# A hybrid encoder trunk on one core: half B's stream tile in the place of the projection's ring, half A's first recurrence chunk starting with the work that needs no inverse, gated outputs loaded by GpSimd's queue, and bonus sums one pair later

## The chip, the cores and the metric

The kernel runs on one core of one Trainium2 chip. TensorE (PE) multiplies, VectorE (DVE), ScalarE (ACT) and GpSimd (POOL) do the element-wise work, and SyncE (SP) does little but issue transfers; ACT and POOL issue some too. The metric is the device time of one execution in microseconds.

## The reference

Two pre-norm layers, each a mixer and a SwiGLU feed-forward (FFN), then a final norm. Width 1024, 1024 tokens, FFN width 2816, all float32. The first mixer is a gated MLP beside mean pooling; the second is RWKV-7, and the change is about that one:

```python
def rwkv7_time_mix(h, mu, w_r, w_k, w_v, w_o, w0, w1, w2, a0, a1, a2, g1, g2,
                   k_k, k_a, r_k, ln_w, ln_b, v_first, vres):
    xx = jnp.pad(h, ((0, 0), (1, 0), (0, 0)))[:, :-1] - h
    xr, xw, xk, xv, xa, xg = [h + xx * mu[i] for i in range(6)]
    r = xr @ w_r
    wlog = -jax.nn.softplus(-(w0 + jnp.tanh(xw @ w1) @ w2).astype(f32)) - 0.5
    k = xk @ w_k
    v = xv @ w_v
    a = jax.nn.sigmoid(a0 + (xa @ a1) @ a2)
    g = jax.nn.sigmoid(xg @ g1) @ g2
    kk = heads(k * k_k)
    kk = kk / jnp.maximum(jnp.sqrt(jnp.sum(kk * kk, axis=-1, keepdims=True)), 1e-12)
    k = k * (1 + (a - 1) * k_a)
    ...
    # per head, over time: state = state * w + (state @ -kk) (kk * a)^T + v k^T ; y = state @ r
    y = wkv7_scan(rh, decay, kh, vh, -kk, kk * ah)
    ...  # per-head norm of y, then:
    bonus = jnp.sum(rh * kh * r_k.astype(f32), axis=-1, keepdims=True) * vh
    y = (y + bonus.reshape(bsz, seq, d)).astype(h.dtype)
    return (y * g) @ w_o, v_first

def swiglu(hn, w_gate, w_up, w_down):
    return (jax.nn.silu(hn @ w_gate) * (hn @ w_up)) @ w_down
```

## The kernel before

The tokens are cut in half A (0 to 511) and half B (512 to 1023). Float32 products are made of three matmuls (`mm3`, L435 to L437; `hi` is the rounded value and `lo` the rest: hi by hi, hi by lo, lo by hi) on tiles of 128 by 512; below these are called dense matmuls. Weights come through a plan (`push`, `take`): a tile `raw` is loaded by ACT's queue (L125), then split by `split`: ACT copies hi (L161), VectorE subtracts to lo (L162). `raw` has a few slots, so a late release holds back later loads. Each transfer of SP and ACT also takes one of eight semaphores in turn (lanes) and waits for the one before on its lane.

For each half, `project` makes the inputs of the RWKV recurrence: per pair of heads `p`, a product for k and one for r, the small products with w2 and a2 (L1385), the sums over a head (`squares`; `bonus`, L1334, which needs k after L1440), and an inverse of a small triangular matrix per head and 32 tokens (`invert`, VectorE), which GpSimd writes to `xi0_d` and `xi_d` (L1519 to L1525). Then `recur` runs over eight chunks of 64 tokens: `gram` (products of the inputs, evicted to gt, L1604), `flip_bk`, `below` and `below2` (combine the parts of the inverse, which SP loads as XT, L1590; copies L1647 and L1648), `own` (what the state gives, Q, L1660), `apply` (L1685, L1686, to uv), the new state, and `out`. Its small matmuls are all at L1562. `post` follows for each two chunks: norm statistics (L1766 to L1776), a power on GpSimd (L440), scaling to L1791 (ysb), PE transposes ("turns") and the gate (L1808, yend for the last two chunks). The gated outputs of the first three pairs of chunks go to `y_d` and are loaded again (yl) for the out-projection with w_o.

Beside each recurrence PE runs FFN work of the other half (dense matmuls with `hid`, `hd`), and `drive` interleaves them: the recurrence yields a cost, and dense work runs for as much, times `ratio`. A scheduler at build time sets the order of each engine from this, and the engines run in that order. Residuals stream in by SP (`in_pieces`, L1946) and are added by VectorE (L534). `recur` opens with:

```python
        load(0)
        ...
        with tc.issue_after(loaded[0].ins):
            stream_loaded = stream()
        with tc.issue_after(stream_loaded):
            load_x(0)
        with tc.issue_after(loaded[0].ins):
            load(1)
            load_x(1)
        yield START * ratio
        ...
        bkt = flip_bk(0)
        w1 = below(0)
```

Of the kernel before, what the change touches and what calls it, by code (L numbers as in the profile page):

```python
# [47 lines left out]
def tile_trunk(  # L48
# [66 lines left out]
    def push(key, parts, view=lambda t: t, dest=None):  # L115
        plan.append((key, parts, view, dest))
# [32 lines left out]
    def take(key):  # L149
        i = pos[0]  # L150
        assert plan[i][0] == key, (plan[i][0], key)
        pos[0] += 1
        split_at(i)
        load_at(i + 1)
        if i + 1 in raws:
            load_at(i + 2)
        split_at(i + 1)
        return ready.pop(i)

    def split(src, hi, lo, eng=None):  # L160
        act.activation(hi, src, AF.Copy)  # L161
        (eng or dve).tensor_tensor(out=lo, in0=src, in1=hi.bitcast(F32), op=ALU.subtract)  # L162

    def stack(los):

        def go(n, src, dst, _):
            act.activation(dst, src, AF.Copy)
            r = los[n]
            dve.tensor_tensor(out=dst[r], in0=src[r], in1=dst[r].bitcast(F32), op=ALU.subtract)

        return go

    splits["wa2"] = stack([slice(64, 128), slice(0, 64)])
    splits["g2b"] = stack([slice(32, 64)])

# [81 lines left out]
    def push_proj(h, nxt=None):  # L257
        push(("r", h, 0), colblk(rwkv_w_r[0], 0))
        push(("g2", h), rowblk(rwkv_g2[0], 0))
        push(("g2b", 0, h), [(lambda raw, i=i: raw[i * 32 : i * 32 + 32], rwkv_g2[0][128:160, :]) for i in range(3)],  # L260
             lambda t: t[:96], lambda: (wst.tile([P, D], F32R, tag="whi", name="whi"),) * 2)
        for n, w in enumerate((rwkv_w2, rwkv_a2)):
            push(("wa2", n, h), [(lambda raw, i=i: raw[i * 64 : i * 64 + 64], w[0]) for i in range(2)],
                 dest=lambda n=n: (dests["wa2"](n),) * 2)
        for m in range(8):
            push(("k", h, m), colblk(rwkv_w_k[0], m * P))
            if m:
                push(("r", h, m), colblk(rwkv_w_r[0], m * P))
        pieces = push_act(*nxt) if nxt else iter(())
        for cb in range(2):  # L270
            for kp in range(4):
                push(("v", h, cb, kp), kpair(rwkv_w_v[0], kp, cb * 512))
                if kp % 2:
                    next(pieces, None)
# [93 lines left out]
    def push_units(units, between=iter(())):  # L368
        for i, n in units:
            push(("first1", i, n), push_pair(1, i, n, 0))  # L370
            next(between, None)
            next(between, None)

    for e in ffn_events(TAIL, True):
        if e == ("d", TAIL[-1]):
            push_units(UNITS[:AHEAD_IN])
        if e[0] != "d":
            push_ffn_event(1, 0, *e)
    push_units(UNITS[AHEAD_IN : AHEAD_IN + 2], push_act(("y", 1), y_d[1], HT - P))
    for go in push_o(1):  # L380
# [39 lines left out]
    def auxt():  # L420
        return pst("aux")
# [719 lines left out]

    rows = [slice(0, 64), slice(64, 128)]
    def project_norm(h, np_, b=None):
# [105 lines left out]
    def project(h, hn1, kp, ring, keep, before_v):  # L1249
# [14 lines left out]
        w2 = tmp("w2", 1, [P, D], F32R), tmp("a2", 1, [P, D], F32R)  # L1264
        dests["wa2"] = lambda n: w2[n]

# [4 lines left out]
        for m in range(KT):  # L1271
# [6 lines left out]
            for r in range(2):  # L1278
                sp.dma_start(g_d[h][rows[m % 2], m // 2 * 2 + r, :], t[rows[r]])
        for n in range(2):  # L1280
            take(("wa2", n, h))

# [82 lines left out]
        def invert_on(n):  # L1365
            while inv and n:
                n -= 1
                if next(inv[0], "end") == "end":
                    inv.pop(0)

        for p in range(KT):
            ms = slice(p * P, (p + 1) * P)

            wk = take(("k", h, p))
            o = mmt()
            dense2(o, *wk, xk)
            invert_on(INV)
# [35 lines left out]
            else:  # L1413
                squares()
            if prev is not None:
                for j in range(4):
                    bonus(prev[0], prev[3], j)
            if p == 3:
# [22 lines left out]
            sp.dma_start(ab_d[h][:, :, 0, p].rearrange("c q s j -> q c s j"), ar)  # L1441
            prev = (p, ar, bk, kt)
        oa = [auxt() for _ in range(2)]

        def bonus_out():
            for j in range(4):
                bonus(prev[0], prev[3], j)
            bs = tmp("rn", 1, [P, 64]).rearrange("t (j r p) -> t j r p", j=4, r=2)
            dve.tensor_copy(bs, bo[:, 0:64].rearrange("t (j p r) -> t j r p", p=8, r=2))
            sp.dma_start(bon_d[h].rearrange("j t r p -> t j (r p)"), bs.rearrange("t j r p -> t j (r p)"))  # L1450
            for r in range(2):
                sp.dma_start(
                    bon[rows[1 - r], h * 8 : h * 8 + 8, :], bon_d[h][:, :, r, :].rearrange("j (c t) p -> t (j c) p", t=64)
                )
# [85 lines left out]
    def recur(h, wp, stream, ratio, end):  # L1540
# [4 lines left out]

        def wt(tag, bufs, shape):
            return wp.tile(shape, F32, tag=tag, bufs=bufs, name=tag)

        def smt():
# [112 lines left out]

        def burst(c, bkt, w1):

# [3 lines left out]
            between()  # L1668
            Q = own(c, S0)
            between()  # L1670
            yield 0.1
            if more:
                gram(c + 1, 0)
                between()
                yield 0.1
# [12 lines left out]
            yield 0.1  # L1688
            if more:
                gram(c + 1, 1)  # L1690
                between()
                yield 0.1
# [126 lines left out]
        with tc.issue_after(loaded[0].ins):  # L1819
            stream_loaded = stream()  # L1820
        with tc.issue_after(stream_loaded):
            load_x(0)
        with tc.issue_after(loaded[0].ins):
            load(1)
            load_x(1)
        yield START * ratio
# [4 lines left out]
        yield 0.5  # L1831
        bkt = flip_bk(0)
        w1 = below(0)
        yield 2.0
        for c in range(8):
            if c % 2 == 1:
                pieces[:] = [post(c // 2)]
                next(pieces[0])
            open_[0] = (99, 1)[c % 2]
            bkt, w1 = yield from burst(c, bkt, w1)  # L1840
            if c < 7 or not h:
                yield BURST
# [24 lines left out]

    def with_first():
        early_o[0] = take(("o", 0, 0))
        for q in range(4):  # L1870
            qs = slice(2 * q, 2 * q + 2)
            split(yl[:, qs, :], *(t[:, qs, : HT - P] for t in ys))
            yield
        split_end(ys, end_a.tiles)

# [239 lines left out]
    for k in range(0, KT, 4):  # L2115
        sp.dma_start(yl[:, k : k + 4, :], y_d[0][:, k : k + 4, : HT - P])
    ys = act_tiles((yhi, y))
# [59 lines left out]

    ps_es = open_psum("psm1", MIXED)
    hp, hp_es = open_pool(name="ha2", bufs=1, side="left")
    wp, wp_es = open_pool(name="wp1", bufs=1, side="left")  # L2180
    f, f_es = open_pool(name="ffn2", bufs=1, side="right")
# [7 lines left out]
    drive(dense_a, recur(1, wp, in_pieces(hp, 0, h_d[0, 1]), RATIO, end_b), RATIO)  # L2189
    for e in (wp_es, hp_es, f_es, ps_es):  # L2190
        e.close()
# [6 lines left out]
    reload(hb_pool, 1, h_d[1, 1])  # L2198
    ys = open_act(("y", 1), xa)
    got_y = take_act(("y", 1))  # L2200

# [180 lines left out]
```

## Time and profile before

| what | value |
| --- | --- |
| median of 3 runs | 2355.64 us (2353.9 to 2358.44) |
| the profiled execution | 2354.72 us, span 2353.0 us |
| mean granted clock of PE | 0.986 |
| DMA | 390.75 MB, mean 166 GB/s |
| half A's recurrence | about 1030 to 1235 us |
| half B's recurrence | about 1572 to 1790 us |

A span is the stretch from the first to the last instruction of the profiled execution. In the profile a row of waits gives the engine and the line that waited, the engine, tile and line (or the transfer) that it waited for, and then us in total, times and the longest. PE is the engine that is busy nearly throughout, so rows of the other engines count only where PE waits for them.

### The profile page before, as it was taken

The numbers are of one execution on the slowest core, as the hardware profiler recorded it, in microseconds if no ns is written. First come the engines' busy times: TensorE is split into PE (matmuls) and PEld (weight loads), VectorE is DVE, ScalarE is ACT, GpSimd is POOL, SyncE is SP. The second block draws the span as 40 slices with busy tenths as digits, with TensorE's granted clock in tenths as the row PEclk, the third lists the DMA queues.
The fourth block names the chain that finished last, engine by engine and source line by source line (L and its number), as shares of the span: only waits on it lengthen the run. The fifth ranks groups of instructions, "written<-read, shape, count | busy, mean of one in ns | idle before, by whom it ended". The sixth has DMA issues, their size and how long they took to land. (4 is left out here: it accounts for less than half of the span.)

```text
span 2353.0 us, 38018 instructions
## 1 busy us (share of the span) xinstructions
PE 2278.9 (97%) x15171; PEld 1864.5 (79%) x15171; DVE 1547.1 (66%) x2500; ACT 956.5 (41%) x1527; POOL 173.5 (7%) x203
## 2 busy tenths in 40 slices
PE   8999999999999999999989999988999999999998
PEld 6888888888888888777778778777877888888886
DVE  6435775565567967767788947765764565776565
ACT  6233444343313665533346654523333443332014
POOL 0200000000000021201100011100110000000002
PEclk9999999999999999999999999999999999999999
DMA  5114473333776475776544565785637674547342
GB/s 185 54 45 139 148 209 100 99 117 108 277 251 213 137 202 140 219 217 180 164 146 135 160 186 141 203 236 152 179 104 232 201 255 143 170 150 261 126 161 99
DMA packets 429089, 390.75 MB, mean 166 GB/s; under 512 B 99376, under 2 KB 360624, under 8 KB 425968
## 3 DMA queue, kind: packets, MB, share of 16 engines
q1 hardware_dynamic: 184176, 207.67, 27.6%
q10 hardware_dynamic: 243072, 175.92, 25.5%
q0 software_dynamic: 1664, 4.73, 0.9%
q8 instruction: 119, 1.95, 0.4%
q14 instruction: 58, 0.48, 0.1%
HBM read 282.20 MB, written 106.04 MB: 165 GB/s over the span
## 5 line engine op out<-in xcount | busy, mean ns | idle before, releaser
L161 ACT ACTIVATE whi<-raw 128x1024 fp32r<-128x1024 f32 (+2 forms) x274 | 265.1, 975 | 412.0 <-PE mm L436 219.8
L162 DVE TENSOR_TENSOR wlo<-raw,whi 128x1024 fp32r<-128x1024 f32 (+2 forms) x274 | 308.2, 1130 | 168.1 <-ACT whi L161 144.9
L436 PE MATMUL mm<-alo,whi 128*128 128x512 f32 x864 | 342.7, 397 | 0.8 <-DVE alo L162 0.8
L435 PE MATMUL mm<-ahi,whi 128*128 128x512 f32 x832 | 333.1, 401 | 8.5 <-ACT ahi L161 5.7
L437 PE MATMUL mm<-ahi,wlo 128*128 128x512 f32 x832 | 329.4, 396 | 1.0 <-DVE wlo L162 1.0
L534 DVE TENSOR_TENSOR h<-h,mm 128x512 f32<-128x512 f32 x268 | 180.0, 683 | 145.4 <-PE mm L437 131.9
L771 PE MATMUL mm<-ahi,whi 128*128 128x512 f32 x536 | 210.5, 393 | 2.5 <-DVE t L899 1.6
L772 PE MATMUL mm<-alo,whi 128*128 128x512 f32 x536 | 208.6, 389 | 0.0
L773 PE MATMUL mm<-ahi,wlo 128*128 128x512 f32 x536 | 205.0, 389 | 0.0
L436 PEld LDWEIGHTS mm<-alo,whi 128*128 128x128 f32 x864 | 163.8, 190 | 37.7 <-issue 2.4
L435 PEld LDWEIGHTS mm<-ahi,whi 128*128 128x128 f32 x832 | 157.9, 190 | 44.8 <-ACT ahi L161 6.2
L437 PEld LDWEIGHTS mm<-ahi,wlo 128*128 128x128 f32 x832 | 157.8, 190 | 37.6 <-issue 2.5
L435 PE MATMUL mm<-hd,dhi 128*128 128x512 f32 x368 | 144.3, 392 | 1.0 <-DVE h L534 1.0
L437 PE MATMUL mm<-hd,dlo 128*128 128x512 f32 x368 | 143.4, 390 | 0.0
L436 PE MATMUL mm<-hd,dhi 128*128 128x512 f32 x368 | 143.2, 389 | 0.0
L771 PEld LDWEIGHTS mm<-ahi,whi 128*128 128x128 f32 x536 | 100.6, 188 | 26.0 <-issue 2.7
L773 PEld LDWEIGHTS mm<-ahi,wlo 128*128 128x128 f32 x536 | 100.6, 188 | 21.1
L772 PEld LDWEIGHTS mm<-alo,whi 128*128 128x128 f32 x536 | 100.6, 188 | 21.1 <-issue 0.5
L161 ACT ACTIVATE dhi<-raw 128x1024 fp32r<-128x1024 f32 x40 | 40.5, 1052 | 171.1 <-PE mm L436 131.4
L161 ACT ACTIVATE hid<-t 128x512 fp32r<-128x512 f32 x58 | 36.5, 629 | 115.4 <-DVE t L869 113.7
L435 PEld LDWEIGHTS mm<-hd,dhi 128*128 128x128 f32 x368 | 69.1, 188 | 16.0 <-DVE h L534 1.4
L437 PEld LDWEIGHTS mm<-hd,dlo 128*128 128x128 f32 x368 | 69.1, 188 | 14.4
(444 smaller groups left out, 4712.4 us busy)
## 6 DMA issues: line engine op xcount, KB each, us to landing
raw<-in_ffn_w_down_dram ACTq DMA_DIRECT2D x76, 512.0 KB
raw<-in_ffn_w_gate_dram ACTq DMA_DIRECT2D x68, 512.0 KB
raw<-in_ffn_w_up_dram ACTq DMA_DIRECT2D x68, 512.0 KB
hid_d<-hid SPq DMA_DIRECT2D x68, 512.0 KB
hd<-hid_d SPq DMA_DIRECT2D x56, 512.0 KB
ar<-ab_d SPq DMA_DIRECT2D x16, 1024.0 KB
raw<-in_ab_w_in_dram ACTq DMA_DIRECT2D x16, 512.0 KB
raw<-in_ab_w_out_dram ACTq DMA_DIRECT2D x16, 512.0 KB
```

The lines of the kernel that those rows point to most:

```text
L161: act.activation(hi, src, AF.Copy)
L162: (eng or dve).tensor_tensor(out=lo, in0=src, in1=hi.bitcast(F32), op=ALU.subtract)
L435: pe.matmul(o, whi, xhi, start=first, stop=False)
L436: pe.matmul(o, whi, xlo, start=False, stop=False)
L437: newest[0] = pe.matmul(o, wlo, xhi, start=False, stop=last).ins
L534: dve.tensor_tensor(out=H[h][:, m, :], in0=H[h][:, m, :], in1=o, op=ALU.add)
L771: pe.matmul(o, wh[:, k, :], x[0][:, k, :], start=st, stop=False, skip_group_check=True)
L772: pe.matmul(o, wh[:, k, :], x[1][:, k, :], start=False, stop=False, skip_group_check=True)
L773: pe.matmul(o, wl[:, k, :], x[0][:, k, :], start=False, stop=k == 3, skip_group_check=True)
```

## The change

- **Half B's tiles.** The pool of the recurrence (`wp1`) is opened ahead of that of h (`ha2`), and four of its tiles (gch, vch, lnw, one ysb) are allocated first, so that h takes memory of the projection's ring instead of the inverse's.
- **The loads' order.** On SP, the loads of chunk 1 (ar, uv, uv; `load(1)`) are issued ahead of those of XT of chunk 0, in both halves, and XT of chunk 0 no longer waits behind the stream.
- **Half A's first chunk.** `own(0)` and both halves of `gram(1)` run between `flip_bk(0)` and `below(0)`, with five more units of dense work.
- **Gated outputs.** GpSimd's queue loads yl, in half B straight to a tile of `xb`, where before they came through four `raw` slots.
- **w2 and a2** share one `raw` tile and one entry of the plan; each is split on its 64 rows.
- **Bonus sums** of a pair are issued within the k product of the pair after the next.

```diff
@@ -161,6 +161,8 @@
 
+    rows = [slice(0, 64), slice(64, 128)]
+
     def stack(los):
@@ -170,7 +172,12 @@
 
-    splits["wa2"] = stack([slice(64, 128), slice(0, 64)])
+    def two(_, src, dst, __):
+        for n, r in enumerate(rows):
+            act.activation(dst[n][r], src[r], AF.Copy)
+            dve.tensor_tensor(out=dst[n][rows[1 - n]], in0=src[r], in1=dst[n][r].bitcast(F32), op=ALU.subtract)
+
+    splits["wa2"] = two
     splits["g2b"] = stack([slice(32, 64)])
@@ -259,9 +266,8 @@
              lambda t: t[:96], lambda: (wst.tile([P, D], F32R, tag="whi", name="whi"),) * 2)
-        for n, w in enumerate((rwkv_w2, rwkv_a2)):
-            push(("wa2", n, h), [(lambda raw, i=i: raw[i * 64 : i * 64 + 64], w[0]) for i in range(2)],
-                 dest=lambda n=n: (dests["wa2"](n),) * 2)
+        push(("wa2", 0, h), [(lambda raw, r=r: raw[r], w[0]) for r, w in zip(rows, (rwkv_w2, rwkv_a2))],
+             dest=lambda: (dests["wa2"](), None))
         for m in range(8):
@@ -376,7 +382,7 @@
             push_ffn_event(1, 0, *e)
-    push_units(UNITS[AHEAD_IN : AHEAD_IN + 2], push_act(("y", 1), y_d[1], HT - P))
+    push_units(UNITS[AHEAD_IN : AHEAD_IN + 2])
     for go in push_o(1):
@@ -1139,7 +1145,6 @@
 
-    rows = [slice(0, 64), slice(64, 128)]
     def project_norm(h, np_, b=None):
@@ -1262,7 +1267,7 @@
         w2 = tmp("w2", 1, [P, D], F32R), tmp("a2", 1, [P, D], F32R)
-        dests["wa2"] = lambda n: w2[n]
+        dests["wa2"] = lambda: w2
 
@@ -1277,8 +1282,7 @@
                 sp.dma_start(g_d[h][rows[m % 2], m // 2 * 2 + r, :], t[rows[r]])
-        for n in range(2):
-            take(("wa2", n, h))
+        take(("wa2", 0, h))
 
@@ -1368,12 +1372,13 @@
 
+        due = []
         for p in range(KT):
...
             o = mmt()
-            dense2(o, *wk, xk)
+            dense2(o, *wk, xk, between=[lambda: None] * 2 + ([due.pop(0)] if len(due) > 1 else []))
             invert_on(INV)
@@ -1412,9 +1417,6 @@
                 squares()
-            if prev is not None:
-                for j in range(4):
-                    bonus(prev[0], prev[3], j)
             if p == 3:
@@ -1440,11 +1442,12 @@
             prev = (p, ar, bk, kt)
+            due.append(lambda p=p, kt=kt: [bonus(p, kt, j) for j in range(4)])
         oa = [auxt() for _ in range(2)]
...
         def bonus_out():
-            for j in range(4):
-                bonus(prev[0], prev[3], j)
+            for go in due:
+                go()
             bs = tmp("rn", 1, [P, 64]).rearrange("t (j r p) -> t j r p", j=4, r=2)
@@ -1544,7 +1547,15 @@
         def wt(tag, bufs, shape):
+            if tag in late_used:
+                return late_used.pop(tag)
             return wp.tile(shape, F32, tag=tag, bufs=bufs, name=tag)
+
+        late_used = {}
+        if h:
+            late_used = {t: wt(t, n, sh) for t, n, sh in (
+                ("gch", 1, [P, 8, P]), ("vch", 1, [P, 2, 8, 64]), ("lnw", 1, [P, 8, 64]), ("ysb", 3, [P, 8, 64]),
+            )}
 
@@ -1660,16 +1671,16 @@
 
-        def burst(c, bkt, w1):
+        def burst(c, bkt, w1, own0=None):
 
...
             between()
-            Q = own(c, S0)
+            Q = own(c, S0) if own0 is None else own0
             between()
             yield 0.1
-            if more:
+            if more and own0 is None:
                 gram(c + 1, 0)
@@ -1686,7 +1697,7 @@
             yield 0.1
-            if more:
+            if more and own0 is None:
                 gram(c + 1, 1)
@@ -1817,12 +1828,11 @@
         with tc.issue_after(loaded[0].ins):
-            stream_loaded = stream()
-        with tc.issue_after(stream_loaded):
-            load_x(0)
+            stream()
+            load(1)
         with tc.issue_after(loaded[0].ins):
-            load(1)
-            load_x(1)
+            for c in range(2):
+                load_x(c)
         yield START * ratio
@@ -1830,6 +1840,15 @@
         bkt = flip_bk(0)
+        own0 = None
+        if h == 0:
+            own0 = own(0, S[0])
+            yield 0.5
+            for q in range(2):
+                gram(1, q)
+                yield 0.5
+            yield 5.0 * ratio
+            last.append(newest[0])
         w1 = below(0)
@@ -1837,7 +1856,7 @@
             open_[0] = (99, 1)[c % 2]
-            bkt, w1 = yield from burst(c, bkt, w1)
+            bkt, w1 = yield from burst(c, bkt, w1, None if c else own0)
             if c < 7 or not h:
@@ -1865,12 +1884,15 @@
 
-    def with_first():
-        early_o[0] = take(("o", 0, 0))
+    def split_y(yl, ys):
         for q in range(4):
...
             yield
+
+    def with_first():
+        early_o[0] = take(("o", 0, 0))
+        yield from split_y(yl, ys)
         split_end(ys, end_a.tiles)
@@ -2113,7 +2135,7 @@
     for k in range(0, KT, 4):
-        sp.dma_start(yl[:, k : k + 4, :], y_d[0][:, k : k + 4, : HT - P])
+        pool.dma_start(yl[:, k : k + 4, :], y_d[0][:, k : k + 4, : HT - P])
     ys = act_tiles((yhi, y))
@@ -2176,8 +2198,8 @@
     ps_es = open_psum("psm1", MIXED)
+    wp, wp_es = open_pool(name="wp1", bufs=1, side="left")
     hp, hp_es = open_pool(name="ha2", bufs=1, side="left")
-    wp, wp_es = open_pool(name="wp1", bufs=1, side="left")
     f, f_es = open_pool(name="ffn2", bufs=1, side="right")
@@ -2187,7 +2209,7 @@
     drive(dense_a, recur(1, wp, in_pieces(hp, 0, h_d[0, 1]), RATIO, end_b), RATIO)
-    for e in (wp_es, hp_es, f_es, ps_es):
+    for e in (hp_es, wp_es, f_es, ps_es):
         e.close()
@@ -2196,8 +2218,12 @@
     reload(hb_pool, 1, h_d[1, 1])
-    ys = open_act(("y", 1), xa)
-    got_y = take_act(("y", 1))
+    xb.tile([P, KT, HT], F32R, tag="ahi", name="ahi")
+    yl = xb.tile([P, KT, HT], F32R, tag="alo", name="yl").bitcast(F32)[:, :, : HT - P]
+    for k in range(0, KT, 4):
+        pool.dma_start(yl[:, k : k + 4, :], y_d[1][:, k : k + 4, : HT - P])
+    ys = act_tiles(xa)
+    got_y = split_y(yl, ys)
 
```

What the build makes of it, at the three places that matter most. Half A's first chunk on PE, before: `gt` is the product tile, `hidhi` and `hidlo` belong to dense work, and the last row is `below`, which needs XT.

```order
L437 MATMUL mm<-hidhi,wlo 128x512
L435 MATMUL mm<-hidhi,whi 128x512
L436 MATMUL mm<-hidlo,whi 128x512
L437 MATMUL mm<-hidhi,wlo 128x512
L435 MATMUL mm<-hidhi,whi 128x512
L436 MATMUL mm<-hidlo,whi 128x512
L1562 MATMUL sm<-XT,gt 32x32 x16
```

The dense row after the flip leads straight to `below`. After: the same engine and place, the end of `own(0)` (uv, S) and the begin of `gram(1)` (ar):

```order
L1573 MATMUL sm<-uv,gt 64x64
L1573 MATMUL sm<-S,ar 64x64
L1573 MATMUL sm<-uv,gt 64x64
L1573 MATMUL sm<-S,ar 64x64
L1573 MATMUL sm<-ar 64x128 x16
L441 MATMUL mm<-hidhi,whi 128x512
L442 MATMUL mm<-hidlo,whi 128x512
```

`below` now follows 43 dense matmuls after the flip, where it was 14.

PE at half A's end, before, where seven of the last eight turns (ident, ysb) are followed by 18 dense matmuls with `hd` and then the out-projection:

```order
L435 MATMUL mm<-hd,whi 128x512
L436 MATMUL mm<-hd,whi 128x512
L437 MATMUL mm<-hd,wlo 128x512
L1562 MATMUL sm<-ident,ysb 128x128 x7
L435 MATMUL mm<-hd,whi 128x512
L436 MATMUL mm<-hd,whi 128x512
L437 MATMUL mm<-hd,wlo 128x512
```

And after:

```order
L441 MATMUL mm<-hd,whi 128x512
L442 MATMUL mm<-hd,whi 128x512
L443 MATMUL mm<-hd,wlo 128x512
L1573 MATMUL sm<-ident,ysb 128x128 x8
L476 MATMUL aux<-small,nacc 128x1 x4
L441 MATMUL mm<-ahi,whi 128x512 x3
L442 MATMUL mm<-alo,whi 128x512
L443 MATMUL mm<-ahi,wlo 128x512
```

The eight turns now stand right ahead of the norm sums (nacc) and the out-projection (ahi), with no dense work of the FFN between.

ACT in half B's first two chunks, before (`wdhi` is the split of w_down):

```order
L161 ACTIVATE wdhi<-raw 128x1024 x2
L125 DMA raw<-in_ffn_w_up_dram 128x8x128
L125 DMA raw<-in_ffn_w_down_dram 128x1024
L1647 ACTIVATE XT<-sm 32x4x32
L161 ACTIVATE wdhi<-raw 128x1024
L1647 ACTIVATE XT<-sm 32x4x32
L1659 ACTIVATE Q<-sm 128x512
```

And after:

```order
L125 DMA raw<-in_ffn_w_up_dram 128x8x128
L1658 ACTIVATE XT<-sm 32x4x32
L125 DMA raw<-in_ffn_w_down_dram 128x1024
L1658 ACTIVATE XT<-sm 32x4x32
L1670 ACTIVATE Q<-sm 128x512
L161 ACTIVATE wdhi<-raw 128x1024
L125 DMA raw<-in_ffn_w_gate_dram 128x8x128
L1696 ACTIVATE uv<-sm 64x512
```

The load of w_down moved from behind the next gate-up loads' splits of chunk 1 to between the two XT copies of chunk 0.

## Prediction

> **What bounds the kernel now.** I read the table of engines first, then what TensorE (PE) waited for over the whole span, then the clock and busy time in the stretches of its long waits, and last the chain that ended last there.
>
> ```profile
> PE 2278.9 (97%) x15171; PEld 1864.5 (79%) x15171; DVE 1547.1 (66%) x2500; ACT 956.5 (41%) x1527; POOL 173.5 (7%) x203
> ```
> ```profile
> PE sm L1562 <- DVE gt L1604: 8.9, 3, 7.5
> PE sm L1562 <- DVE XT L1648: 6.7, 2, 6.4
> ...
> PE mm L435 <- ACT ahi L161: 5.7, 1, 5.7
> PE sm L1562 <- DMA XT<-xi_d: 5.3, 1, 5.3
> PE sm L1562 <- DVE ysb L1791: 3.6, 4, 1.2
> PE bo L1334 <- DVE k L1440: 3.2, 2, 2.8
> PE mm L435 <- ACT whi L161: 2.7, 2, 2.3
> ...
> PE aux L1385 <- DVE a L169: 1.9, 1, 1.9
> ...
> PE mm L437 <- DVE wlo L162: 1.0, 2, 0.5
> ```
>
> PE is busy for 2278.9 of 2353.0 us, so 74 us are idle, and only two things can be won: that idle time, and the clock lost after it. The rows are engine, line, what it waited for, total, times, longest: six waits of 2.3 to 7.5 us, all in or beside the two recurrences. The next table gives, for the stretch of each long wait and the one behind it, length, busy time per engine, PE's granted clock, DMA share and GB/s.
>
> ```profile
> 1037.00:1043.00 6.00, 0.73 (x8) 0.30 (x11) 0.69 (x1) 0.00 (x0) 0.00 (x0) 0.89 1.03 255
> 1043.00:1049.00 6.00, 6.00 (x46) 4.79 (x47) 1.37 (x2) 0.39 (x2) 0.00 (x0) 0.54 0.78 188
> 1207.00:1227.00 20.00, 19.46 (x90) 15.73 (x89) 18.02 (x41) 7.76 (x15) 2.90 (x1) 1.00 0.38 114
> 1227.00:1235.00 8.00, 2.60 (x12) 1.82 (x10) 8.00 (x16) 4.74 (x7) 0.20 (x1) 0.87 1.00 310
> 1235.00:1241.00 6.00, 5.65 (x16) 4.50 (x17) 5.85 (x8) 3.76 (x6) 0.00 (x0) 0.61 0.97 294
> 1354.00:1360.00 6.00, 5.55 (x24) 3.95 (x23) 1.23 (x1) 3.82 (x8) 0.00 (x0) 1.00 0.92 257
> 1383.00:1389.00 6.00, 5.49 (x17) 4.72 (x18) 4.07 (x6) 3.46 (x7) 1.28 (x2) 0.50 0.72 172
> 1572.00:1580.00 8.00, 0.48 (x6) 0.38 (x3) 2.32 (x4) 0.00 (x0) 0.00 (x0) 0.64 0.70 259
> 1580.00:1586.00 6.00, 6.00 (x22) 4.86 (x20) 2.74 (x5) 1.20 (x2) 0.00 (x0) 0.63 1.06 314
> 1617.00:1623.00 6.00, 3.99 (x96) 3.58 (x96) 5.91 (x16) 2.79 (x4) 0.00 (x0) 0.58 0.33 94
> 1793.50:1800.00 6.50, 6.50 (x17) 5.05 (x18) 3.43 (x4) 2.50 (x3) 0.00 (x0) 0.54 0.96 264
> ```
>
> So a wait costs twice: itself, and up to (1 - clock) x 6 us behind it. Since small matmuls lose less than the dense ones, I take three quarters of that: 2.1 us after the wait at 1037 (0.54), 1.7 at 1580 (0.63), 1.9 at 1617 (0.58), 2.2 at 1793 (0.54, 6.5 us). The 1.9 us wait at 1351 left the clock at 1.00; the 2.8 us wait at 1380 and the pair of 2.3 and 0.5 at 1790 did not (0.50, 0.54). The Trainium skill ("TensorE: Matmul & The Clock Gate", "Why this matters for your kernels") puts the limit at idle gaps of about 3 us. By that the waits at 1380 and 1790 would have cost no clock, and my sum would be 3.3 us smaller in gain, 2336; the rows show the loss, so the rows decide. The dense pace is 90 matmuls in 19.46 us, 0.216 us each.
>
> **Half A's first chunk (gain 7.4).** The wait for XT at 1037 is the whole time that `below(0)` stands ready with its inverse not loaded. In before, 14 dense matmuls stand between `flip_bk` and `below`. Now there are `own(0)` (32 small), both `gram(1)` (32 small) and 43 dense ones: 29 more dense, 6.3 us, and 64 small ones, priced by two rows of the chain that ended last (start, length, count):
>
> ```profile
> 1591.34 0.44 PE sm L1562 x32
> ...
> 1593.17 1.10 PE sm L1562 x30
> ```
>
> So they take 0.9 to 2.3 us. The added cover of 7.2 to 8.6 us exceeds the wait of 5.3; 5.3 + 2.1 = 7.4 go. Two new waits stand on this path: `own` needs S, cleared by GpSimd early, and `gram(1)` needs ar of chunk 1, 1 MB whose issue moves on SP from behind the XT loads to ahead of them. It now travels while PE does the flip. Were it late, up to the 5.3 would come back; I take 0, range 0 to 4.
>
> **Half A's end (loss 4).** What moved in front must be missing at the end: between the last `out` of chunk 7 (1207.0) and the out-projection there stood 90 dense matmuls, now 60, that is 13.0 us instead of 19.5. Beside them runs a chain of VectorE, GpSimd and ACT, here some of its rows (start, length, what):
>
> ```profile
> 1212.39 0.17 DVE L1776 TENSOR_SCALAR var<-var 128x16 f32<-128x16 f32 x1
> ...
> 1222.16 0.68 DVE L1791 TENSOR_TENSOR ysb<-ysb,vch 128x512 f32<-128x512 f32 x1
> ...
> 1226.29 2.15 DVE L1808 SCALAR_TENSOR_TENSOR yend<-sm,vec,gch 128x128 f32<-128x128 f32 x8
> ...
> 1233.69 1.22 DVE L162 TENSOR_TENSOR wlo<-raw,whi 128x1024 fp32r<-128x1024 f32 x1
> ```
>
> ysb is ready at 1222.84, 15.8 us after 1207; the eight yend take 2.15; norm additions and the weight splits between them (1.22 each) follow, and VectorE is busy for 18.02 of 20 us. In before PE then waited 5.7 us more, for ahi, because the gated outputs' load stood behind the spills of h on SP. That load goes to GpSimd's queue and is issued near 1207 + 14, so at some 7 us (a rival below prices it) it is no longer last. Behind it on GpSimd stands only the power for the norm sums (L440), which is wanted later. With VectorE's new order I count ysb done 16.6 to 18.9 us after the last `out`, yend at about 23, the norm sums (which now stand ahead of the out-projection) at 26, the out-projection at 26 to 27.4 against 28.35 before. Work in between is 14.8 us with the turns: 11 to 12.6 idle, if nothing overlaps; by parts 9 to 12 against 6.3 to 6.9 (the 5.7 and small ones beside it). Loss 2 to 6 with the clock, taken 4. The work that left is done elsewhere, so nothing else is lost.
>
> **Half B's start (gain 8.2).** The chain that ended last shows it, with the second stall behind it; SP's row names the reason:
>
> ```profile
> 1564.41 9.19 DMA xi_d<-xi
> 1573.74 3.82 DMA h<-h_d
> ...
> 1598.20 8.12 DMA lnw<-in_rwkv_ln_w_dram
> 1606.39 9.12 DMA raw<-in_ffn_w_down_dram
> 1615.54 1.06 ACT wdhi L161
> 1616.63 1.23 DVE wdlo L162
> ```
> ```profile
> SPq L1946 <- DMA xi_d<-xi: 18.2, 4, 10.6
> ```
>
> The stream's load of h (L1946) lay on the inverse's memory and could be issued only when GpSimd's writes of it had landed; then VectorE's residual (L534) waited for h, and gt (L1604) stood behind it in order. With wp1 opened ahead of ha2, h lies on the projection's ring, whose readers are long done: it waits only for its DMA lanes, and lands some 8 us earlier. 7.5 + 1.7 = 9.2 go. Next in line is XT of chunk 0, loaded after those same writes land (1573.7) and now behind the second ar and uv on SP: at h's 3.82 us or somewhat more it lands at 1577 to 1580, while flip and the 26 dense matmuls end near 1579. Residue 0 to 4, taken 1.
>
> **Half B's second stall (gain 5.8).** w_down was issued at 1606.39, when the slow lnw load had landed, took 9.12 us, and its split (ACT, then VectorE) stood ahead of XT's copy: 6.4 + 1.9 = 8.3. The new ACT order issues it between the two XT copies of chunk 0, ahead of lnw, gch and vch, at about 1586 by the earlier start; landing between h's 3.8 us and its own 9.1 later, 1590 to 1595. The split now stands ahead of uv (L1685), for which PE has cover until 1592. Residue 0 to 5, taken 2.5.
>
> **w2 and a2 in one tile (gain 1.9).** Two DMAs and one slot instead of four and two; the splits are four halves instead of four full ones. The row `a L169` is 1.9 in half B; the second load that it waited for is gone. Range 1 to 2.3.
>
> **Bonus sums (gain 2.5).** The wait on k (2.8 at 1380) is met by six more dense matmuls, 6 x 0.216 = 1.3 us; what is left, 1.5, is under the 1.9 that left the clock alone, so half of the clock's 3.0 x 0.75 goes as well: 1.3 + 1.2. Ends 0.7 and 5.
>
> **Half B's gated outputs (gain 4.5).** In before they took four slots of the weights' ring, so that w_o came late; start and length of ACT's rows:
>
> ```profile
> 1783.91 1.56 ACTq L125 DMA_DIRECT2D raw<-in_rwkv_w_o_dram  x2
> ...
> 1790.97 1.06 ACT L161 ACTIVATE whi<-raw 128x1024 fp32r<-128x1024 f32 x1 [0.80 <-DMA raw<-in_rwkv_w_o_dram]
> ...
> ```
>
> Now w_o starts behind the last gch load, and the outputs come by two GpSimd DMAs, issued over 20 us ahead of the turns. 2.3 + 0.5 + 2.2 = 5.0. The cover from the last `out` to the turns falls from 126 dense to 70 (15.1 us), against 15.8 for the same chain in half A and less here: residue 0 to 3, taken 0.5. The Trainium skill ("DMA: Bandwidth & Descriptors", "Issuing engines are not separate DMA queues") says that transfers from any queue share the same 16 engines, so that another queue saves only issue time. If the queue were the point of this part, its gain would be 0 and the sum 2337; here the freed slots are the point, and the stretch 1227 to 1235 (DMA share 1.00) agrees that the engines are the limit.
>
> **Elsewhere.** In the recurrences small waits (ysb 3.6 in four) stand in a new order; between -1 and 6, taken 3 lost.
>
> **Sum.** -7.4 + 4 - 8.2 - 5.8 - 1.9 - 2.5 - 4.5 + 3 = -23.3. The profiled execution took 2354.7 us (span and 1.7), 0.9 under the median: 2331.4 there, 2332 as a median.
>
> **Rivals.** *The inverse sets half B's pace.* XT lands late behind ar and w_down: of 9.2 + 8.3, half comes back beyond my residues, 5 to 9 us: 2337 to 2345. For it: GpSimd's inverse writes took 9.19 us and end at 1573.7 whatever h does. Against: 26 dense matmuls now stand there. *Half A's end costs 12, not 4*: VectorE is at 18 of 20 us there, and cover is a third less: 2340. *The load on GpSimd's queue is slow* (the other side): software DMAs of before move small blocks only; 0.5 MB took
>
> ```profile
> xi_d<-xi POOLq DMA_DIRECT2D x1, 512.0 KB, 6.9
> ```
>
> 6.9 us. Two of 0.77 MB in turn would be 21 us at that pace, landing at 1207 + 35: a stall 8 us longer than forecast, 2340. Slower than before comes out from 23.3 + 4.7 = 28 us of further lateness, at 1207 + 55, half the pace of that row: 2360 and more. *The waits only change names*, because each is followed by another as long (the inverse in A, XT in B, ysb at both ends): 2355.
>
> **How the numbers follow.** Forecast 0.64 (2324 to 2340), inverse 0.16, half A's end 0.08, only names 0.06, slow queue 0.06. About 0.2%, 4.7 us, is what a measurement can tell from no change: the first three are faster, less 0.02 of their tails: faster 0.86, same 0.08, slower 0.06. All gains at their full size with the smallest losses give -35, 2321; all at their small end -1. I cut at 2321 and 2348, which leaves out the last two and a small part of the rest.
>
> **What would show it.** Right: no XT wait at A's `below`, clock 1.00 from there on; a PE wait of 9 to 12 us ahead of A's out-projection, on yend, not yl; no gt wait of 7.5 and no XT wait of 6.4 in B; no whi wait ahead of B's out-projection. Wrong: PE idle near 74 us again, with XT, S or ar in the rows; or GpSimd's load as what ended a wait.

## The result, and the profile after

The changed kernel takes 2329.7 us (median of 4 runs, 2324.2 to 2330.7), against 2354.8 for the kernel before in its four: ratio 0.9896, 95% interval 0.9861 to 0.9931. Forecast were 2332 us, from 2321 to 2348. The profiled execution has a span of 2327.4 us, 25.6 less than before. PE's row, and what PE waited for:

```profile
PE 2270.2 (98%) x15171; PEld 1855.4 (80%) x15171; DVE 1547.3 (66%) x2500; ACT 957.1 (41%) x1527; POOL 181.7 (8%) x207
```
```profile
PE aux L593 <- DMA vrow<-in_mix_norm_dram: 6.4, 1, 6.4
PE sm L1573 <- DVE ysb L1802: 5.8, 4, 2.1
PE aux L476 <- DVE nacc L455: 5.4, 1, 5.4
PE sm L1573 <- DMA XT<-xi_d: 5.2, 1, 5.2
PE aux L1308 <- DVE bk L1437: 2.5, 2, 1.7
PE yp L1573 <- issue: 1.9, 2, 1.5
PE sm L1573 <- DVE gt L1615: 1.8, 3, 0.7
```

Idle time is 2327.4 - 2270.2 = 57.2 us, where it was 74.1: 16.9 less. PE's busy time fell by 8.7 with the same instructions, and the mean granted clock rose from 0.986 to 0.992. (Lines behind the edits stand 6 to 26 higher than before; L1573 is the old L1562.) The gt wait of 7.5, the XT wait of 6.4 on VectorE, the ahi wait, the whi wait of 2.3 and the a wait are gone. New are 5.4 on nacc and 4.2 on ysb in two waits, all at half A's end, and the wait for an XT load is now in half B. The same columns as before (length, PE, PEld, DVE, ACT, POOL, clock, DMA share, GB/s), for the changed places:

```profile
1037.00:1043.00 6.00, 6.00 (x132) 4.34 (x134) 2.92 (x5) 0.60 (x1) 0.00 (x0) 1.00 0.81 222
1043.00:1049.00 6.00, 6.00 (x72) 4.63 (x62) 4.77 (x6) 2.29 (x3) 0.00 (x0) 1.00 0.68 182
1224.00:1237.00 13.00, 3.43 (x17) 2.81 (x17) 11.22 (x22) 5.73 (x9) 3.47 (x3) 0.69 0.88 243
1237.00:1243.00 6.00, 6.00 (x16) 4.54 (x17) 4.34 (x6) 1.58 (x2) 1.69 (x1) 0.53 0.20 39
1570.00:1577.00 7.00, 1.83 (x39) 1.26 (x37) 0.69 (x1) 0.00 (x0) 0.00 (x0) 0.77 0.58 152
1577.00:1583.00 6.00, 6.00 (x22) 4.80 (x20) 1.14 (x2) 1.82 (x3) 0.00 (x0) 0.70 0.02 5
1765.00:1785.00 20.00, 20.00 (x90) 16.57 (x89) 11.55 (x13) 9.94 (x13) 0.00 (x0) 1.00 0.86 277
```

PE is busy throughout half A's start at full clock, waits for 9.6 us in 13 at A's end (3.43 busy; 4.2 for ysb, 5.4 for nacc) with the clock at 0.53 behind that, waits for 5.2 at B's start, and is busy for 20 of 20 us around B's out-projection.

Summed over windows of 2 us, PE's idle time by stage in this kernel and the later ones (A start 1020 to 1060 us, A end 1190 to 1250, B's projection 1340 to 1400, B start 1540 to 1630, B end 1730 to 1800), with the ratio to the kernel before:

| kernel | A start | A end | B's projection | B start | B end | ratio, 95% |
| --- | --- | --- | --- | --- | --- | --- |
| before | 5.3 | 6.3 | 5.4 | 15.1 | 2.8 | 1 |
| changed | 0.3 | 9.9 | 0.0 | 7.8 | 0.0 | 0.9896 (0.9861 to 0.9931) |
| changed, run again | 1.0 | 9.5 | 1.1 | 5.9 | 0.0 | 0.9912 (0.9888 to 0.9936) |
| `no_first` | 4.8 | 2.7 | 0.0 | 8.4 | 4.8 | 0.9925 (0.9911 to 0.9938) |
| `no_tiles` | 0.0 | 10.1 | 0.0 | 10.4 | 0.0 | 0.9931 (0.9915 to 0.9947) |
| `xt_mid` | 0.0 | 9.5 | 0.0 | 5.1 | 0.0 | 0.9908 (0.9892 to 0.9924) |
| `xt_mid_short` | 0.0 | 8.5 | 0.9 | 5.2 | 4.6 | 0.9922 (0.9907 to 0.9938) |
| `xt_pool` | 0.0 | 9.5 | 1.2 | 3.6 | 0.1 | 0.9924 (0.9898 to 0.995) |
| `y1_raw` | 0.0 | 9.5 | 1.3 | 3.4 | 3.0 | 0.9931 (0.991 to 0.9953) |
| `yl_sp` | 0.0 | 10.7 | 0.0 | 8.6 | 4.9 | 0.9954 (0.9941 to 0.9967) |
| `no_small` | 0.0 | 11.1 | 3.6 | 6.5 | 4.8 | 0.9969 (0.9953 to 0.9986) |
| `p_nofirst` | 8.3 | 2.7 | 1.0 | 7.0 | 0.0 | 0.9925 (0.9906 to 0.9945) |
| `p_u2` | 0.0 | 8.5 | 0.0 | 8.1 | 0.0 | 0.9904 (0.9883 to 0.9924) |
| `p_u0` | 1.2 | 8.6 | 1.1 | 10.7 | 0.0 | 0.9931 (0.9911 to 0.995) |

A ratio's interval is 0.3 to 0.7% wide, 6 to 16 us, so the stages tell more than the times. The stages come from one execution each.

Idle time at a few places is not the whole time of a stage, so the next rows take whole stretches: first three of the kernel before, then the same three of the changed kernel, in the same columns. Each begins and ends at a matmul that has the same matmuls (by names and shapes) ahead of it in both orders: half A from its first product of `gram` to the first product with ghi in half B's projection; from there, the projection to half B's first `gram`; from there, half B to the next norm sums (nacc).

```profile
1031.30:1349.23 317.93, 301.51 (x3619) 242.34 (x3619) 243.74 (x449) 147.00 (x249) 30.42 (x25) 0.98 0.56 158
1349.23:1570.13 220.90, 213.19 (x1199) 173.89 (x1197) 152.59 (x261) 112.05 (x177) 38.33 (x47) 0.98 0.68 186
1570.13:1846.68 276.55, 254.62 (x3375) 207.95 (x3375) 156.06 (x315) 89.37 (x161) 20.33 (x8) 0.95 0.60 172
```
```profile
1030.38:1350.62 320.24, 303.72 (x3620) 241.90 (x3620) 246.93 (x452) 148.00 (x250) 36.54 (x28) 0.98 0.55 158
1350.62:1561.99 211.37, 208.78 (x1198) 171.00 (x1196) 152.93 (x262) 111.00 (x176) 39.38 (x47) 0.99 0.72 196
1561.99:1821.44 259.45, 249.44 (x3375) 202.77 (x3375) 153.91 (x313) 90.08 (x161) 21.77 (x10) 0.99 0.61 179
```

Half A takes 2.3 us longer than before, with idle time of 16.5 us (320.24 - 303.72) where it was 16.4, and PE 2.2 us longer busy. The projection is 9.5 us shorter and half B 17.1. In the second run of the changed kernel the three stretches are 319.6, 215.0 and 257.0 us.

### The profile page after: what moved, and what is told of

Same layout as the page of the kernel before. It is cut to its first block, busy times and chain, and to the rows that moved or that the text cites. A ratio compares the mean times of both kernels' runs of the same rounds, so it can differ in the third digit from the quotient of the medians.

```text
span 2327.4 us, 37995 instructions
## 1 busy us (share of the span) xinstructions
PE 2270.2 (98%) x15171; PEld 1855.4 (80%) x15171; DVE 1547.3 (66%) x2500; ACT 957.1 (41%) x1527; POOL 181.7 (8%) x207
## 4 chain that ended last, share of the span: by engine, by line
PE 80%; DVE 11%; DMA 5%; issue 2%; ACT 1%; POOL 1%; SPq 0%; ACTq 0%; POOLq 0%; DVEq 0%
PE mm L441 14%; PE mm L442 14%; PE mm L443 14%; PE mm L777 9%; PE mm L779 9%; PE mm L778 9%; PE sm L1573 4%; DVE wlo L162 2%; DVE it L1513 1%; DVE xi L1518 1%; PE yp L1573 1%; DMA raw<-in_ffn_w_gate_dram 1%; PE mm L627 1%; PE mm L628 1%; PE mm L629 1%
## 5 line engine op out<-in xcount | busy, mean ns | idle before, releaser
L777 PEld LDWEIGHTS mm<-ahi,whi 128*128 128x128 f32 x536 | 100.6, 188 | 25.6 <-issue 3.2
```

The lines of the kernel that those rows point to most:

```text
L777: pe.matmul(o, wh[:, k, :], x[0][:, k, :], start=st, stop=False, skip_group_check=True)
```

## Experiments

**XT between ar and uv, and a shorter first chunk.** Theory: the load of half B's XT is late because of what stands ahead of it on SP.

```diff
         stream()
-        load(1)
+        load(1, lambda: load_x(0))   # XT(0) between ar and uv of chunk 1
```

> The changed kernel, but in both halves XT of chunk 0 is loaded between ar and uv of chunk 1, so that the uv loads (which waited some 13 us for their lane, behind a load of gate weights) no longer stand ahead of it on SP. Theory Q (SP's order holds XT of half B): the 5.2 us wait for XT at half B's start falls under 1 us and the clock behind it stays at 1.00; some 6.5 us less than the changed kernel, 2323, ratio 0.987 to before. Rival W (the inverse's writes land late, whatever stands on SP): the wait stays between 4 and 6 us and the time within 2 us of the changed kernel. Half A has no wait there in either case; XT should be issued near 1036 instead of 1043.5.

XT's wait was 3.4 us where 5.2 or, in the second run, 4.4 stood, so neither number came. SP's waits in 1540 to 1582 us, in the changed kernel first, say why; in the second, XT's own load is what waits:

```profile
SPq L1592 <- DMA raw<-in_ffn_w_gate_dram: 21.3, 2, 13.7
```
```profile
SPq L1603 <- DMA raw<-in_ffn_w_gate_dram: 13.2, 1, 13.2
```

In the one kernel uv (L1592) waits for a load of gate weights, in the other XT (L1603) does, at the same position in the order. What binds is the lane that this position gets. Theory Q, that the uv loads hold XT, is wrong; rival W is not shown either. The time, 2329.8 us, is the changed kernel's, where theory Q had 2323. In half A XT was issued at 1035.3, as expected.

```diff
-            yield 5.0 * ratio
+            yield 2.0 * ratio
```

> As xt_mid, and half A's first chunk has 2 instead of 5 extra units of dense work (23 instead of 42 dense matmuls between flip and below). Theory: the dense work that stands in front in half A is missing at its end; 19 matmuls (4.3 us) go back there, so the idle time at A's out-projection falls from 9.9 to 6 to 8 us and no XT wait appears at A's start, since XT is now loaded 7 us earlier: 2 to 4 us less than xt_mid, 2320. Rival (VectorE's queue, not PE's cover, sets the out-projection's start at A's end, so more cover only fills idle time that stays as long after the last matmul): the same 2 to 4 us less, but with the start of the out-projection unmoved against the last chunk's end; if instead VectorE's work moves too, no gain.

A's end has 8.5 us idle instead of 9.5 (6 to 8 expected), now as one wait on ahi. New waits of 4.3 for ysb stand at half B's end, so the ratio is no better: 2333.1 us, where 2320 was expected. By whole stretches, half A is 314.0 us, 5.1 less than in `xt_mid`, and half B 262.5, 5.4 more.

**Half A's first chunk undone.** (Only own, gram and the units; XT ahead of chunk 1 in half A.)

```diff
-        if h == 0:
-            own0 = own(0, S[0])
-            ...
-            yield 5.0 * ratio
```

> The changed kernel without own(0), gram(1) and the five units ahead of below(0) in half A, and with XT of chunk 0 loaded ahead of chunk 1 there as before. The forecast's terms: 7.4 us lost at the start (a wait for XT of about 5 us, clock 0.5 behind it), 4 us won back at A's end (idle 9.9 to about 6.5): together 3.4 us slower than the changed kernel, 2333. Rival (the part is worth nothing, the wait had gone by other means): no wait at A's start, and the time 3 to 4 us less, 2326.

The time is where the forecast's terms had it (2333.9 us; ratio 0.9925 against 0.9896 and 0.9912, with intervals that overlap), but not for their reason. In half A the sum of idle time is 7.5 us without this part and 10.2 to 10.5 with it: 4.5 saved at the start, 7.2 given at the end. The whole stretch of half A is 314.9 us without it, 4.7 to 5.3 less than in the two runs of the changed kernel. Without it, the load of yl is issued early; rows of GpSimd, the changed kernel first:

```profile
1224.23 1.90 POOL L1154 COPY hn<-small 128x8 f32<-128x8 f32 x1 [5.32 <-PE mm L443]
1226.07 1.63 POOL L2138 DMA_DIRECT2D yl<-y_d  x2
```
```profile
1213.26 1.63 POOL L2132 DMA_DIRECT2D yl<-y_d  x2
1232.45 0.19 POOL L1154 COPY hn<-small 128x8 f32<-128x8 f32 x1 [17.56 <-PE mm L443]
```

With the part, the load stands behind a copy that waits for PE's last FFN matmul, which the shifted order puts ahead; PE waits for this load in neither. What made `no_first` slower is half B (267.3 us, 7.9 to 10.3 more), above all its end, where the turns wait for ysb:

```profile
PE sm L1573 <- DVE ysb L1802: 4.8, 2, 3.7
```

This wait is there in `no_first`, `xt_mid_short`, `yl_sp` and `no_small`, and in none of the others: the build orders half B's end otherwise when something far ahead moves.

**Half B's memory as before.**

```diff
...
-    wp, wp_es = open_pool(name="wp1", bufs=1, side="left")
     hp, hp_es = open_pool(name="ha2", bufs=1, side="left")
+    wp, wp_es = open_pool(name="wp1", bufs=1, side="left")
```

> The changed kernel with half B's pools in the old order and no tiles allocated first, so that h again lies on the inverse's memory; the order of loads stays the new one. Forecast's term: h waits for the inverse's writes again, VectorE's residual and gt behind it, 7 to 10 us of PE wait at half B's start in place of the 5.2 for XT: 2 to 6 us slower than the changed kernel, 2332 to 2336. The second stall (6.4 us, w_down) stays away, since the order of w_down's load on ACT is the new one here too. Rival (both stalls of half B go back to where h lies): the 6.4 returns as well, 2338 to 2342.

SP's and PE's rows, in the same stage:

```profile
SPq L1968 <- DMA xi_d<-xi: 18.2, 3, 9.0
```
```profile
PE mm L441 <- DVE h L540: 6.1, 1, 6.1
```

The load of h waits for the inverse again, and PE for VectorE's residual, 6.1 us (less than the 7 to 10 expected; the time, 2334.7, is as expected); the stage is 2.6 to 4.5 us worse, and XT's wait is gone, since both are late together. The second stall stays away: where h lies has nothing to do with w_down. The forecast's reading of both holds.

**Half B's gated outputs through the weights' ring.**

```diff
...
-    pool.dma_start(yl[:, k : k + 4, :], y_d[1][:, k : k + 4, : HT - P])
...
+    got_y = take_act(("y", 1))
```

> The changed kernel with half B's gated outputs loaded by ACT through four slots of the weights' ring again. Theory (the slots hold back w_o): a PE wait of 2 to 3 us for whi at half B's out-projection returns, clock 0.5 behind it, 4.5 us slower than the changed kernel (2334). Rival (the transfers only changed queue): no such wait, within 1 us.

```profile
PE mm L441 <- ACT whi L161: 2.9, 2, 2.4
```

The wait for whi is back, 2.4 at B's out-projection; B's end has 3.0 us idle where the changed kernel has none. The slots were the point. The dip of the clock did not come back with the wait: from 1768 to 1780 us the clock is 1.00, so this run shows 3.0 of the 4.5 us. The ratio, 0.9931, agrees with 4.5 but does not show it alone. This kernel is the same as the changed one at half B's start, and yet PE waited 0.6 us for XT there, not 5.2. Two things differ. The gate weights' load took 7.3 us, not 12.8, so that XT was issued 2.0 us earlier (1570.18); and PE came to half B's first product 3.4 us later (1565.41, not 1561.99). So that stall differs from execution to execution, with the time of that load and with PE's own.

**Half A's gated outputs by SP.**

```diff
-        pool.dma_start(yl[:, k : k + 4, :], y_d[0]
+        sp.dma_start(yl[:, k : k + 4, :], y_d[0]
```

> The changed kernel with half A's gated outputs loaded by SP's queue again, behind the spills of h. Theory (VectorE's queue sets the start of A's out-projection, the load is hidden behind it): idle time at A's end within 1.5 us of the changed kernel's 9.9. Rival (the load on SP lands last): a wait on ahi, 2 to 5 us more there.

A's end has 10.7 us idle against 9.9 and 9.5, within the first theory's 1.5: 5.0 on nacc, 4.2 on ysb and only 1.2 on ahi. The time is 2339.6 us, 10 more than the changed kernel's. The rest of its 0.9954 lies in half B, with XT (6.2) and ysb at the end.

**Both small parts undone** (w2 and a2 apart, bonus sums at their old place).

```diff
...
-            dense2(o, *wk, xk, between=[lambda: None] * 2 + ([due.pop(0)] if len(due) > 1 else []))
+            dense2(o, *wk, xk)
```

> The changed kernel with w2 and a2 in two raw tiles and the bonus sums at their old place. Theory by the forecast's terms: the wait on a (1.9 us) and a wait on k of 2.8 us in half B's projection return, clock 0.5 behind the second: 4.4 us slower, 2334. Rival (both waits had gone because the work ahead of them moved for other reasons): neither returns, within 1 us.

```profile
PE bo L1335 <- DVE k L1441: 2.0, 1, 2.0
PE aux L1387 <- DVE a L171: 1.4, 1, 1.4
```

Both waits return in half B's projection, 3.6 us idle there; the projection's stretch is 218.4 us, 3.4 to 7.0 more than in the two runs of the changed kernel, about the 4.4 of the forecast. This kernel also waits 7.4 for ysb and 3.2 for ndg at A's end and 4.8 at B's end, so its 2341.7 us (2334 expected) and 0.9969 overstate the two parts.

**XT by GpSimd's queue.** It is on none of the lanes that SP and ACT share.

```diff
-                loaded[0] = sp.dma_start(C[c][4][rows[r]], src
+                loaded[0] = (sp if c else pool).dma_start(C[c][4][rows[r]], src
```

> The changed kernel with XT of chunk 0 loaded by GpSimd's queue in both halves, straight behind its own writes of the inverse and on none of the eight lanes that SP and ACT share. Theory L (the lane holds XT: in the run with XT ahead of uv the XT load itself waited 13.2 us for a load of gate weights): XT is issued before 1565 in half B and the 5.2 us wait goes to under 1, the clock behind it stays up; 5 to 7 us less than the changed kernel, 2323. Rival W (the writes of the inverse land late): issue after 1568 all the same, wait 4 to 6 us.

```profile
1553.94 2.21 POOL L1528 DMA_DIRECT2D xi_d<-xi  x2
1556.14 1.38 POOL L1601 DMA_DIRECT2D XT<-xi_d  x2
```

XT is issued at 1556, right behind the last writes, where SP issued it at 1572 in the changed kernel, and PE does not wait for it. So in the changed kernel the lane held XT: what XT of chunk 0 reads is `xi0_d`, whose writes are the first three of six, and there they had landed by 1555.7. But the inverse's other, larger writes are not cleared by this run:

```profile
XT<-xi_d POOLq DMA_DIRECT2D x2, 192.0 KB, 13.6
```

Behind those writes on GpSimd's queue XT took 13.6 us from issue to landing, and PE's first product with it stands at 1570.62, some 0.1 us behind: it came just in time. In the three kernels below with XT on that queue it took 12.4, 14.0 and 14.6 us, each time landing 1 to 3 us behind the last of the larger writes, and in `p_u0` PE waited 2.5 us for it. Whether these writes hold it or the DMA engines, whose share is 1.02 from 1556 to 1570 us in `xt_pool`, no run separates. So the lane is what held XT, and without it the next limit is close behind.

Theory L's time of 2323 did not come: 2332.4 us, the changed kernel's within the intervals. B's start still has 3.6 us idle, of which 2.7 on w, as w_down's load moved behind both XT copies in ACT's order and took 9.2 us.

**The last call, side by side.**

> The changed kernel itself, run beside the next three on one chip so that they can be compared with it. 2330 within 5 us; its waits should be those of its first profile (9 to 10 us idle at A's end, none at A's start), but the wait for XT at half B's start may be anything from 0 to 6 us if the load of gate weights on its lane takes another time.

> XT of chunk 0 by GpSimd's queue, and half A's first chunk as before (no own, gram or units ahead of below). Theory N (the first chunk's part only moves A's idle time from its start to its end): 2 to 5 us of wait for XT at A's start, 1 to 3 us idle at A's end instead of 9.6; with no wait for ysb at B's end, 3 to 6 us less than the changed kernel. Rival (the forecast's terms: 7.4 against 4): 3 us slower than the changed kernel.

> XT of chunk 0 by GpSimd's queue, and 2 instead of 5 units ahead of below in half A; the norm sums of A's end stand behind 20 dense matmuls of the out-projection in the order built. Theory: no wait at A's start (XT lands by 1043), 5 to 8 us idle at A's end, 2 to 5 us less than the changed kernel. Rival (VectorE's queue sets A's end whatever the cover): idle 8 to 10 there, within 2 us of xt_pool.

> XT of chunk 0 by GpSimd's queue, and own(0) and gram(1) ahead of below in half A but no extra unit. Theory: XT lands 1 to 2 us after gram(1) ends, a wait of 0 to 2 us at A's start, 4 to 7 us idle at A's end; 3 to 6 us less than the changed kernel. Rival as for the run with 2 units.

`after_again` came out as expected: 2329.4 us, 9.5 us idle at A's end, 1.0 at A's start (on gt) and 4.4 for XT at half B's start.

`p_nofirst` has 8.3 us idle at A's start and 2.7 at its end, 11.0 together where the changed kernel has 10.5: as theory N says, the part moves the idle time. The 3 to 6 us less of theory N did not come: 2332.7 us is 3.3 slower, the rival's number, with intervals that overlap. With XT on GpSimd the first chunk waits longer (8.3, not 4.8).

`p_u2` has nothing at A's start and 8.5 at its end (5 to 8 expected, 8 to 10 by the rival); 2326.7 us against 2329.4 of the changed kernel on the same chip, intervals overlapping. Its half A is 313.9 us, 4.9 less than that of `xt_pool`, which differs only in the units: as in `xt_mid_short`, 2 units in the place of 5 make half A 5 us shorter.

`p_u0` waits 1.2 us at A's start, as expected, but has 8.6 idle at A's end (4 to 7 expected), and with 2334.0 us it is 4.6 slower than the changed kernel where 3 to 6 less were expected. Behind that wait of 1.2 us the clock was 0.50 from 1046 to 1054 us, and half A takes 325.0 us.

In `p_u2`, `p_u0` and `p_nofirst` the second stall of half B is back, 6.3, 6.8 and 5.5 on XT's copy. ACT's rows of `p_u2`:

```profile
1585.90 0.37 ACTq L125 DMA_DIRECT2D raw<-in_ffn_w_down_dram  x1
...
1595.20 1.06 ACT L161 ACTIVATE wdhi<-raw 128x1024 fp32r<-128x1024 f32 x1 [11.75 <-DMA raw<-in_ffn_w_down_dram]
1596.16 0.25 ACT L1658 ACTIVATE XT<-sm 32x128 f32<-32x128 f32 x1
```

It is the picture of before: w_down's load goes out behind lnw, gch and vch, its split stands ahead of XT's copy. So the second stall goes with ACT's order, and not with where h lies. `xt_pool` has the same order of loads in the source and not this stall; why the build orders ACT otherwise there is open. None of these versions beats the changed kernel by more than the interval.

## Why the prediction was right

The sum was -23.3 for the profiled execution and came out at -25.6 (spans). Term by term, idle time by the stages, clock by the rows of windows:

- *Half A's first chunk, -7.4.* 5.0 idle and the clock dip behind it went; right in size. The forecast that XT has 7.2 to 8.6 us of new cover was right by luck: SP issued XT at 1043.5, not at 1036, since uv waited for its lane there too. PE's product with it stands some 4.4 us behind that issue; at half B's start, where PE waited, it stood 4.2 behind. So there was hardly anything to spare.
- *Half A's end, +4.* Idle time grew by 3.6 and the clock behind it fell from 0.61 to 0.53 over 6 us, 0.4 by the forecast's rule: 4.0. The wait is 4.2 on ysb and 5.4 on nacc, the norm sums' additions on VectorE, which was busy for 11.2 of 13 us; the forecast had named VectorE's queue and the norm sums, and has the out-projection where it came, 27.4 us after the last `out`. Its step on yl was wrong: issued at 1226.1, 16.4 us after the last `out`, not 14, though PE did not wait for it.
- *Half A as a whole.* By these two terms half A should be 3 us shorter. Its whole stretch is 2.3 us longer (1.7 in the second run). So the forecast's step "The work that left is done elsewhere, so nothing else is lost" did not hold: idle time in the stretch is what it was, and PE was busy 2.2 us longer, for a reason that no run here shows. `no_first` and the two kernels with 2 units have half A at 313.9 to 314.9 us, less than before's 317.9: as built, with 5 units, this part lost time. With XT on GpSimd's queue it did not (318.8 us in `xt_pool`, 320.5 in `p_nofirst`).
- *Half B's start, -8.2.* The 7.5 for gt went, but 5.2 for XT came in its place where a residue of 1 was taken (0 to 4 allowed): the term that was mis-sized. The forecast looked at the inverse's last writes, which XT of chunk 0 does not read, and at SP's order, and missed the lane.
- *Second stall, -5.8.* 6.4 and its clock went almost whole; the residue of 2.5 did not come. w_down landed in 4 us, not 9.
- *w2 and a2, -1.9, and bonus sums, -2.5.* B's projection fell from 5.4 to 0 or 1.1 us idle, and the clock stays at 1.00: some 6, more than 4.4. The whole stretch is 9.5 us shorter, 5.9 in the second run; with both parts undone (`no_small`) it is 2.5 shorter than before, so not all of this is theirs.
- *Half B's gated outputs, -4.5.* 2.8 idle and the dip to 0.54 went: 5.0. The loads were issued 10 us ahead of the turns (1748.69, the turns at 1758.89), not over 20, and PE did not wait for them.
- *Elsewhere, +3.* Outside the stages idle time is 74.1 - 34.9 = 39.2 before and 57.2 - 18.0 = 39.2 after: 0. Outside the three stretches the time is 1.3 us shorter.

By whole stretches the forecast was -3.4 for half A, -4.4 for the projection, -18.5 for half B and +3 elsewhere; they came out at +2.3, -9.5, -17.1 and -1.3. So each wait that was to go went, and the sum is close in part by luck: what half A lost against the forecast, the projection and the rest won. The rival "the inverse sets half B's pace" was right that XT is next; the lane was the cause in the changed kernel, and the inverse's writes come into it only with XT on GpSimd's queue. (Its 5 to 9 us give 2337 to 2341, not 2345; and the ends of the terms add up to -36 and -4, not -35 and -1.) The slow queue did not come: the y_d loads on GpSimd's queue landed within 5.9 to 10.4 us, and PE waited for them in neither half.

The rule on the clock fits where the forecast used it: behind 9.6 us of waits at A's end it is 0.53, behind 5.2 at B's start 0.70. As a rule on the length of one wait it does not hold. In `y1_raw` the wait of 2.4 us left the clock at 1.00; in `p_u0` one of 1.2 us was followed by 0.50. The changed kernel itself has a wait of 1.7 us for bk at 1475, with 0.50 from 1478.2 to 1481.6, and the kernel before has one of 1.5 us at 1493, with 0.66 from 1495 to 1500. So the 1.9 us that left the clock alone in the forecast's rows was no safe length, and what else decides is open.

## What to carry to other kernels

When a wait at the head of a chain is covered by work taken from its tail, price both ends with the clock, since here 4.5 us won at the start cost 7.2 at the end. Then compare the whole stretch between two matmuls that both orders share: idle time at its two ends said 3 us won, the stretch 2.3 lost. When a load is late, look at what the issuing row itself waits for: here it was neither the data nor the queue's order but a lane shared with a weight load of 12.8 us, and changing places on the queue only changed which load waited. Where a build orders the engines, an edit moves waits hundreds of microseconds away, so undo each part and compare stages, not only times.

## What was not expected of the hardware

A 512 KB load of weights took 12.8 us (1558.1 to 1570.9) beside the inverse's writes, h and ar; the same load took 11.9 us in the second run and 7.3 in `y1_raw`, and loads of w_down of the same size took 4.0 in the changed kernel and 9.2 in `xt_pool`. On GpSimd's queue 192 KB took 12.4 to 14.6 us behind the inverse's writes. A copy of 128 by 8 on GpSimd took 1.90 us in the changed kernel and 0.19 in `no_first`.
